# Retention heads on one Trainium2 core: six value and gate groups as seven-product pairs

## The chip, the cores and the metric

The kernel runs on one core of one Trainium2 chip. The core has a matrix engine (TensorE, PE in the profile, its weight loads PEld), VectorE (DVE), ScalarE (ACT), GpSimd (POOL) and SyncE (SP), which run side by side, each through its own queue in order. Transfers are issued from the queues of SP, ACT and POOL. The metric is the device time of one execution in microseconds (us), lower is better.

## The reference

A trunk of two layers over 256 tokens of width 2048: gated linear attention, then retention, each with a pre-norm, a gate path and a residual add, and a final norm. The change is in the retention layer:

```python
def retention_mixer(h, positions, w_in, gn_g, gn_b, w_out):
    proj = h @ w_in                       # 2048 -> 2048 q, 2048 k, 4096 v, 4096 gate
    q, k, v, gate = jnp.split(proj, [RET_DK, 2 * RET_DK, 2 * RET_DK + D_INNER], axis=-1)
    q, k = apply_rotary(q, cos, sin), apply_rotary(k, cos, sin)
    # 8 heads of 256 key and 512 value columns:
    #   o = (decayed causal scores of q, k) @ v, normed per head, * gn_g + gn_b
    return (o * jax.nn.silu(gate)) @ w_out
```

All of it is float32. The kernel keeps that precision by splitting each operand in two.

## The kernel before

**Split operands.** A number is held as a rounded high part `hi` and the rest `lo`. A product is three matmuls: high by high, high by `lo`, low by `hi`, each of 128 x 128 by 512 columns. Activations are held split for good: `xhl` (the normed layer input, transposed, 16 blocks of 128 of the contraction) and `ogt` (the gated head outputs). Weights are split as they stream in.

**Weights.** All weight matrices stand in `w_all` as groups of 512 columns, 16 blocks deep, in the order of use. `plan_all` lists once, ahead of the program, which chunks (4 blocks, 1024 KB, one load on SP into one of 4 `raw` buffers) and which units (2 blocks, half a chunk) are used in which order. `emit_split` splits one unit: ScalarE copies `raw` to `hi` (L207), VectorE writes `lo` = `raw` - `hi` (L208). `next_weights` keeps two units split ahead of the one in use; `hi` and `lo` have three buffers each.

**A head of retention** (`ret_head`) is three groups: `group_w` for the query and key columns (`rqk`), `group_x` for the value (`rv`) and for the gate (`rg`). `group_x` takes 8 units, each with 2 blocks x 2 token halves x 3 matmuls. `evac_w` copies the query/key sums out of PSUM (L411, L412), `ret_scores` makes rotary and scores, `o_mms` multiplies scores by values, a norm follows, `og_part` multiplies by the gate and `transpose_out` writes `ogt`. Heads 0 to 3 are followed by half of the output projection (`out_half`, `ra`), 4 to 7 by the other half (`rb`).

**Output halves** already use seven products. `pair_x` takes two groups of 512 columns at once. The first 8 of 16 blocks of the contraction form a 2 x 2 by 2 x 2 block product (two halves of the contraction, two token halves, two groups) which is made with 7 products (blocks S1 to S7, 2 units and 12 matmuls each) instead of 8; the other 8 blocks are done plainly (V0 to V3 for the first group, G0 to G3 for the second, 1 unit and 12 matmuls each). The sums of activations are made by `token_combos` on VectorE; the sums of weights are made by the transfer: once a unit of an S block is split, POOL issues a load of 512 KB that adds another chunk into the same `raw` buffer (L216). `join` adds a product into the residual tile `resid` as soon as it is done.

**Side work.** Generators in the queue `side` hold the work that isn't weights; `advance` runs one step of the first one after each unit or block, `drain_side` the rest. The order in each engine's queue is set by a scheduler when the program is built, from that order and from priorities. PSUM has 4 banks `acc`, 2 `lev`, 2 `mis`.

Of the kernel before, what the change touches and what calls it, by code (L numbers as in the profile page):

```python
# [17 lines left out]
P = 128  # L18
# [37 lines left out]
def kernel(  # L56
# [19 lines left out]
    one = pool("one", 1)  # L76
    raw_p = pool("raw", 4)
# [32 lines left out]
    def plan_units(c, last=True, then=()):  # L110
        for half in range(per_raw):
            units.append((c, half, last and half == per_raw - 1, then))
# [5 lines left out]
    PAIR = ("S1", "S2", "V0", "V1", "S5", "S3", "V2", "G0", "S6", "G1", "S7", "V3", "S4", "G2", "G3")  # L118

    def plan_pair(gp, gq):  # L120
# [7 lines left out]
        for block in PAIR:  # L128
            kind, n = block[0], int(block[1])
            if kind in "VG":  # L130
                j, half = divmod(n, 2)
                c = chunk(kind + str(j), gp if kind == "V" else gq, 2 + j)
                units.append((c, half, half == 1, ()))
            elif n == 2:
                plan_units(plan_chunk(gp, 1))
            elif n in (3, 7):
                plan_units(chunk("y", gq, 1), n == 7, [(gq, 0)] if n == 3 else ())
            else:
                then = {1: [(gq, 0)], 5: [(gq, 1)], 6: [(gp, 1)], 4: ()}[n]
                plan_units(chunk("x", gp, 0), n == 4, then)  # L140

    def plan_all():
        g = 0
        for stage, heads in (("gla", 2), ("gla", 2), ("ret", 4), ("ret", 4)):
            for _ in range(heads * (5 if stage == "gla" else 3)):
                plan_group(g)
                g += 1
            plan_pair(g, g + 1)
# [3 lines left out]
            else:  # L152
                plan_pair(g + 2, g + 3)
# [41 lines left out]
    def emit_split(pieces=1, between=None):  # L195
# [9 lines left out]
        for k in range(pieces):  # L205
            sl = slice(k * step, (k + 1) * step)
            a = nc.scalar.activation(hi[:, sl], src[:, sl], AF.Copy)  # L207
            b = nc.vector.tensor_tensor(lo[:, sl], src[:, sl], hi[:, sl].bitcast(F32), ALU.subtract)  # L208
            if i == 0:
# [4 lines left out]
        for g, k in then:  # L214
            rows = slice(j * SUB, (j + 1) * SUB)
            nc.gpsimd.dma_start(src, chunk_src(g, k)[:, rows], accum_op=ALU.add)  # L216
# [4 lines left out]
    state = {"sub": 0}  # L221
    side = deque()

    def advance(n=1):
        for _ in range(n):
            while side:
                try:
                    next(side[0])
# [37 lines left out]
    def product(ps, a, hi, lo, q, start, stop):  # L266
        xh, xl = a
        mm(ps, xh, hi[:, q, :], start=start, stop=False, skip_group_check=True)
        mm(ps, xh, lo[:, q, :], start=False, stop=False, skip_group_check=True)
        mm(ps, xl, hi[:, q, :], start=False, stop=stop, skip_group_check=True)  # L270

    def token_combos(lhs, name):
# [12 lines left out]
        for half in range(2):  # L285
# [9 lines left out]
            d = v_p.tile([P, 2, 2, CHUNK, P], F32R, tag="v", name=f"{name}_d{half}")  # L295
# [5 lines left out]

    combos = {}

    def pair_x(lhs, name, cname, join, done):

        a = lev_p.tile([P, GW], F32, tag="lev", name=f"{name}_psa")
        c11 = acc_p.tile([P, GW], F32, tag="acc", name=f"{name}_ps11")

        def seven(ps, get, start, stop):
            for half in range(2):  # L310
                hi, lo = next_weights()
                for q in range(SUB):
                    k = half * SUB + q
                    product(ps, get(k), hi, lo, q, start and k == 0, stop and k == CHUNK - 1)
# [5 lines left out]
        def mixed(n):  # L320
            return lambda k: tuple(x[:, k] for x in combos[cname][n])

        def both(ps, j, start, stop):
            hi, lo = next_weights()
            for q in range(SUB):
                for t in range(2):
                    kt = 2 * CHUNK + j * SUB + q
                    x = tuple(lhs[:, kt, i, t * P : (t + 1) * P] for i in range(2))
                    product(ps[t], x, hi, lo, q, start[t] and q == 0, stop[t] and q == SUB - 1)
            advance()  # L330

        c21 = b = c12 = c22 = None
        for block in PAIR:
            kind, n = block[0], int(block[1])
            if kind == "V":
                if c21 is None:
                    c21 = acc_p.tile([P, GW], F32, tag="acc", name=f"{name}_ps21")
                if n == 2:
                    drain_side()
                both((c11, c21), n, (False, n == 0), (n == 3, False))  # L340
                if n == 3:
                    done(0, 0, c11)
            elif kind == "G":
                if c22 is None:
                    c22 = lev_p.tile([P, GW], F32, tag="lev", name=f"{name}_ps22")
                both((c12, c22), n, (False, n == 0), (n == 3, n == 3))
                if n == 3:
                    done(0, 1, c12)
                    done(1, 1, c22)
            elif n == 1:  # L350
                seven(a, plain(0, 0), True, True)
                join(0, 0, a, ALU.add)
            elif n == 2:
                seven(c11, plain(1, 0), True, False)
            elif n == 5:
                while cname not in combos:
                    advance()
                b = lev_p.tile([P, GW], F32, tag="lev", name=f"{name}_psb")
                seven(b, mixed(0), True, True)
                join(0, 1, b, ALU.subtract)  # L360
                join(1, 1, b, ALU.add)
            elif n == 3:
                c12 = acc_p.tile([P, GW], F32, tag="acc", name=f"{name}_ps12")
                seven(c12, mixed(2), True, False)
            elif n == 6:
                seven(a, mixed(1), False, True)
                join(0, 1, a, ALU.subtract)
            elif n == 7:
                seven(a, mixed(3), False, True)
                join(1, 0, a, ALU.subtract)  # L370
                join(1, 1, a, ALU.add)
            elif n == 4:
                seven(c21, plain(1, 1), False, True)
                done(1, 0, c21)

    def group_w(rhs, name, extra=None):
        ps = [acc_p.tile([P, 2, SEQ], F32, tag="acc", name=f"{name}_ps{c}") for c in range(4)]
        for j in range(NSUB):
# [3 lines left out]
            if last:  # L382
# [19 lines left out]
            if extra is not None:  # L402
                extra(j)
            advance()
        return ps

    def evac_w(ps, dst, name):
        tmp = t4_p.tile([P, 4, SEQ], F32, tag="t4", name=f"{name}_h2")
        with tc.high_priority():
# [22 lines left out]
    resid = const([P, 2, D], "resid")  # L432
# [85 lines left out]
    def square_sum(t, c):  # L518
        junk = sg_p.tile([P, GW], F32, tag="sg", name="sqj")
        nc.scalar.activation(  # L520
            junk, resid[:, t, c * GW : (c + 1) * GW], AF.Square, accum_out=ssum[:, t, c : c + 1]
# [36 lines left out]
    def gate_low_rank():  # L558
        for t in range(2):
            keep(nc.sync.dma_start(resid[:, t, :], x_n[:, t, :]))  # L560
# [42 lines left out]
    def o_mms(sc, v, name):  # L603
        ps = [acc_p.tile([P, GW], F32, tag="acc", name=f"{name}_ps{t}") for t in range(2)]
# [11 lines left out]
    def transpose_out(src, kt0, scale0, dst, name):  # L616
        for half in range(2):
# [7 lines left out]
            for jj in range(2):  # L625
                kt = kt0 + half * 2 + jj
                if scale0 is None:
                    nc.scalar.activation(dst[:, kt, 0, :], tp[:, jj, :], AF.Copy)
                    nc.vector.tensor_tensor(
                        dst[:, kt, 1, :], tp[:, jj, :], dst[:, kt, 0, :].bitcast(F32), ALU.subtract  # L630
                    )
                else:
# [127 lines left out]
    def gla_head(h):  # L760
# [22 lines left out]
        def o_part(gi):  # L783
# [9 lines left out]
            if gi == 1:  # L793
                side.append(og_part(0))
                if h % 2:
                    side.append(token_combos(ogt, "gb" if h == 3 else "ga"))
# [48 lines left out]
    def out_cols(c, ps, t, first, final):  # L845
        dst = resid[:, t, c * GW : (c + 1) * GW]
# [8 lines left out]
    def out_half(first, final, name, later=None):  # L855
        def finish(t, c, ps):
# [3 lines left out]
            for _ in transpose_out(  # L860
                lambda t, j: resid[:, t, c * GW + j * P : c * GW + (j + 1) * P],
# [7 lines left out]
        for pair in range(1 if final else 2):  # L869
# [5 lines left out]
            def join(t, n, ps, op):  # L875
                c = 2 * pair + n
                dst = resid[:, t, c * GW : (c + 1) * GW]
                with tc.high_priority():
# [318 lines left out]
```

## Time and profile before

| what | value |
|---|---|
| median of 3 runs | 1400.7 us (1400.02 to 1400.75) |
| profiled execution, its own time | 1400.51 us |
| its span, first to last instruction | 1398.7 us |
| granted TensorE clock | 0.998 of full |
| TensorE busy / weight loads busy | 1385.4 us (99%) / 1163.1 us (83%) |
| VectorE, ScalarE, GpSimd busy | 999.6, 746.9, 100.0 us |
| HBM read / written | 285.51 MB / 2.10 MB |
| unit splits: L207 on ScalarE, L208 on VectorE | 515 each, 1058 and 1221 ns |

A row of a group reads: source line, engine, operation, output tile <- input tiles, shape, count | busy time in us, mean ns of one | idle time just before them and what ended it. Lines are those of the kernel before. Buffer numbers are left out of tile names.

### The profile page before, as it was taken

To read this page: it belongs to the slowest core of one execution; us is meant where nothing else is said; L and a number is where in the kernel's file an instruction comes from. 1 tells how busy PE (TensorE), PEld (TensorE's weight loads), DVE (VectorE), ACT (ScalarE), POOL (GpSimd) and SP (SyncE) were. 2 spreads that over 40 slices of the span, in tenths; PEclk is the share of its full clock that TensorE was granted. 3 is DMA by queue.
4 is the path that set the end of the run, shared out by engine and by line. 5 is a ranking of instruction groups with operands and counts; after the bars stand their busy time and mean duration, and the time that the engine had idled before them with its cause. 6 is when DMAs were issued, how large, how long until landed. Compare 5 with 4: busy or idle time off the path is not lost.

```text
span 1398.7 us, 17710 instructions
## 1 busy us (share of the span) xinstructions
PE 1385.4 (99%) x6716; PEld 1163.1 (83%) x6716; DVE 999.6 (71%) x1531; ACT 746.9 (53%) x954; POOL 100.0 (7%) x155
## 2 busy tenths in 40 slices
PE   8999999999999999999999999999999999999997
PEld 7888888788888888888888888888888888888887
DVE  6595798787845784887766666687766666668783
ACT  6665656655554646666444444456544444444563
POOL 1001030110010020111000000001100000000200
PEclk9999999999999999999999999999999999999999
DMA  9554555898555555799555555569975555555981
GB/s 365 196 181 150 191 182 180 199 298 261 178 179 181 178 194 183 193 281 281 184 191 189 191 190 190 182 195 269 265 250 179 201 181 200 183 200 177 232 298 60
DMA packets 47205, 288.75 MB, mean 206 GB/s; under 512 B 5632, under 2 KB 6144, under 8 KB 17296
## 3 DMA queue, kind: packets, MB, share of 16 engines
q1 hardware_dynamic: 35808, 249.71, 51.0%
q0 software_dynamic: 10304, 36.57, 13.2%
q10 hardware_dynamic: 1008, 1.35, 0.3%
q8 instruction: 52, 0.85, 0.2%
q14 instruction: 33, 0.27, 0.1%
HBM read 285.51 MB, written 2.10 MB: 206 GB/s over the span
## 4 chain that ended last, share of the span: by engine, by line
PE 98%; DVE 1%; ACT 1%; DMA 0%; issue 0%; ACTq 0%; DVEq 0%
PE rqk_ps L400 8%; PE gv_ps L247 4%; PE gg_ps L247 4%; PE gv_ps L248 4%; PE rv_ps L248 4%; PE rv_ps L249 4%; PE rv_ps L247 4%; PE gg_ps L248 4%; PE gv_ps L249 4%; PE gg_ps L249 4%; PE rg_ps L249 4%; PE rg_ps L248 4%; PE rg_ps L247 4%; PE rqk_ps L401 4%; PE gqk_ps L400 4%; PE gqk_ps L401 2%
## 5 line engine op out<-in xcount | busy, mean ns | idle before, releaser
L208 DVE TENSOR_TENSOR lo<-raw,hi 128x1024 fp32r<-128x1024 f32 (+1 forms) x515 | 623.9, 1221 | 307.7 <-ACT hi L207 305.3
L207 ACT ACTIVATE hi<-raw 128x1024 fp32r<-128x1024 f32 (+1 forms) x515 | 543.4, 1058 | 537.8 <-PE rg_ps L249 97.9
L400 PE MATMUL rqk_ps<-xhl,hi 128*128 128x512 f32 x480 | 167.3, 398 | 0.0
L401 PE MATMUL rqk_ps<-xhl,lo 128*128 128x256 f32 x480 | 127.3, 280 | 0.0
L400 PEld LDWEIGHTS rqk_ps<-xhl,hi 128*128 128x128 f32 x480 | 89.0, 188 | 18.0
L248 PE MATMUL rv_ps<-lo,xhl 128*128 128x512 f32 x256 | 100.4, 392 | 0.0
L248 PE MATMUL gv_ps<-lo,xhl 128*128 128x512 f32 x256 | 100.4, 392 | 0.0
L248 PE MATMUL gg_ps<-lo,xhl 128*128 128x512 f32 x256 | 100.4, 392 | 0.0
L249 PE MATMUL gv_ps<-hi,xhl 128*128 128x512 f32 x256 | 100.3, 392 | 0.0
L249 PE MATMUL gg_ps<-hi,xhl 128*128 128x512 f32 x256 | 100.0, 391 | 0.0
L249 PE MATMUL rv_ps<-hi,xhl 128*128 128x512 f32 x256 | 99.7, 390 | 0.0
L248 PE MATMUL rg_ps<-lo,xhl 128*128 128x512 f32 x256 | 99.6, 389 | 0.0
L249 PE MATMUL rg_ps<-hi,xhl 128*128 128x512 f32 x256 | 99.6, 389 | 0.0
L247 PE MATMUL gv_ps<-hi,xhl 128*128 128x512 f32 x256 | 93.0, 391 | 0.0
L247 PE MATMUL rg_ps<-hi,xhl 128*128 128x512 f32 x256 | 91.8, 389 | 0.0
L247 PE MATMUL gg_ps<-hi,xhl 128*128 128x512 f32 x256 | 91.7, 391 | 0.0
L247 PE MATMUL rv_ps<-hi,xhl 128*128 128x512 f32 x256 | 91.7, 390 | 0.0
L401 PEld LDWEIGHTS rqk_ps<-xhl,lo 128*128 128x128 f32 x480 | 89.1, 189 | 3.1
L400 PE MATMUL gqk_ps<-xhl,hi 128*128 128x512 f32 x216 | 72.4, 396 | 0.0
L216 POOL DMA_DIRECT2D raw<-in_w_all x56 | 48.3, 862 | 294.8 <-DVE lo L208 276.7
L248 PEld LDWEIGHTS rg_ps<-lo,xhl 128*128 128x128 f32 x256 | 48.0, 188 | 10.0
L247 PEld LDWEIGHTS rg_ps<-hi,xhl 128*128 128x128 f32 x256 | 48.1, 188 | 10.0
(412 smaller groups left out, 2482.9 us busy)
## 6 DMA issues: line engine op xcount, KB each, us to landing
raw<-in_w_all SPq DMA_DIRECT2D x231, 1024.0 KB, 4.9
raw<-in_w_all POOLq DMA_DIRECT2D x56, 512.0 KB, 7.4
resid<-in_x_n SPq DMA_DIRECT2D x2, 1024.0 KB, 10.9
gg<-in_gn_g POOLq DMA_DIRECT2D x8, 256.0 KB, 3.8
gb<-in_gn_b POOLq DMA_DIRECT2D x8, 256.0 KB, 4.5
raw<-in_w_all SPq DMA_DIRECT2D x3, 512.0 KB, 6.6
xt<-in_x_t SPq DMA_DIRECT2D x3, 512.0 KB, 8.2
dm<-in_dmat POOLq DMA_DIRECT2D x8, 192.0 KB, 2.7
```

The costliest lines, as they stand in the source:

```text
L207: a = nc.scalar.activation(hi[:, sl], src[:, sl], AF.Copy)
L208: b = nc.vector.tensor_tensor(lo[:, sl], src[:, sl], hi[:, sl].bitcast(F32), ALU.subtract)
L216: nc.gpsimd.dma_start(src, chunk_src(g, k)[:, rows], accum_op=ALU.add)
L247: mm(ps, xh, hi[:, q, :], start=kt == 0, stop=False)
L248: mm(ps, xh, lo[:, q, :], start=False, stop=False)
L249: mm(ps, xl, hi[:, q, :], start=False, stop=kt == NKT - 1)
L400: mm(ps[c], wh, rhs[:, kt, :, :], start=kt == 0, stop=False)
L401: mm(ps[c][:, 0, :], wl, rhs[:, kt, 0, :], start=False, stop=False)
```

## The change

In each half of the retention layer the first three heads (0 to 2 and 4 to 6) make value and gate together as one pair with seven products; heads 3 and 7 keep the two plain groups.

- `plan_all` and `plan_pair` list the chunks and units of those pairs, with an order of blocks `RET` that puts V0 ahead of S2.
- `token_combos` is also run on `xhl`, once in each half (`x1`, `x2`). Its split results stay for three heads in the buffer of the residual tile (`res_p`). For that time the residual (2048 KB) is stored to DRAM (`held`) at the end of the output half, from POOL, and loaded back in head 3 and head 7.
- `pair_x` gives each finished product to a handler `on`. For the heads the handler puts products into the `o` and `sg` tiles: S1, S5 and S7 are copied by ScalarE, the others added by VectorE. In output halves the product of S5 stays in its PSUM bank as the start of the fourth sum, which takes one `join` out of each of the seven pairs.
- The score-by-value product, the norm and the gate of a paired head move into the next head's query/key group (`late_o`, banks `lev`).
- From the first retention head on, each side step is queued behind the two latest split instructions (`behind_splits`), and the steps of `ret_scores` and of the norm are cut smaller. `transpose_out` evacuates two blocks in one instruction where there is no scale.

```diff
-    PAIR = ("S1", "S2", "V0", "V1", "S5", "S3", "V2", "G0", "S6", "G1", "S7", "V3", "S4", "G2", "G3")
+    OUT = ("S1", "S2", "V0", "V1", "S5", "S3", "V2", "G0", "S6", "G1", "S7", "V3", "S4", "G2", "G3")
+    RET = ("S1", "V0", "S2", "V1", "S5", "S3", "V2", "G0", "S6", "G1", "S7", "V3", "S4", "G2", "G3")
...
+            latest[:] = [a.ins, b.ins]
...
+    @contextmanager
+    def behind_splits():
+        with tc.issue_after(latest[0]), tc.issue_after(latest[1]):
+            yield
...
-                    next(side[0])
+                    with behind_splits() if state["behind"] else nullcontext():
+                        next(side[0])
...
-            d = v_p.tile([P, 2, 2, CHUNK, P], F32R, tag="v", name=f"{name}_d{half}")
+            d = room(half)
...
+    def room_res(name):
...
+                t.append(res_p.tile([P, 2, 2, 2, CHUNK, P], F32R, tag="resid", name=f"{name}_d"))
...
+        if keep_resid:
+            nc.gpsimd.dma_start(held, R["t"])
...
+        def on(event, ps, shared=True):
+            if event == "p1":
+                with tc.high_priority():
+                    nc.scalar.activation(o[:, 1, :], ps, AF.Copy)
+            elif event == "q":
+                with tc.high_priority():
+                    nc.scalar.activation(sg[:, 0, :], ps, AF.Copy)
+            elif event == "p2":
+                with tc.high_priority():
+                    tt(sg[:, 0, :], ps, sg[:, 0, :], ALU.add)
+            elif event == "p3":
+                with tc.high_priority():
+                    nc.scalar.activation(o[:, 0, :], ps, AF.Copy)
+            elif event == "11":
+                with tc.high_priority():
+                    tt(o[:, 1, :], ps, o[:, 1, :], ALU.add)
+                split_scaled(v[:, 0], o[:, 1, :], r2[:, 0:1])
+            elif event == "21":
...
+            else:
+                t = int(event[0]) - 1
+                with tc.high_priority():
+                    tt(sg[:, t, :], ps, (o if t else sg)[:, 0, :], ALU.add if t else ALU.subtract)
+                keep(nc.scalar.activation(sg[:, t, :], sg[:, t, :], AF.Silu, scale=r[:, t : t + 1]))
...
+        pair_x(xhl, f"rp{h}_", "x1" if h < 4 else "x2", on, RET)
...
+            new_resid(f"resid{h}")
+            nc.gpsimd.dma_start(R["t"], held)
...
-    out_half(False, False, "gb")
+    out_half(False, False, "gb", keep_resid=True)
+    side.append(token_combos(xhl, "x1", room_res("x1")))
     for h in range(4):
         ret_head(h)
-    out_half(True, False, "ra")
+    out_half(True, False, "ra", keep_resid=True)
+    side.append(token_combos(xhl, "x2", room_res("x2")))
```

The order on the engines, at three places. Tile numbers are those of each program, and brackets name what the instruction waits for. First, ScalarE where the query/key group of head 1 ends, before: `hi280` and `hi281` are the first two units of the value group, split ahead, `rqk1_h2` the copies of the query/key sums, `hi282` the value group's third unit.

```order
L207 ACTIVATE hi280_6313<-raw124_6227 128x1024 [waits DMAHW5_49,DVE_49,PE_49]
L207 ACTIVATE hi281_6333<-raw124_6227 128x1024 [waits DVE_49,PE_49]
L411 ACTIVATE rqk1_h2_6354<-rqk1_ps0_6161 128x256 [waits PE_49]
L411 ACTIVATE rqk1_h2_6354<-rqk1_ps1_6162 128x256 [waits PE_49]
L411 ACTIVATE rqk1_h2_6354<-rqk1_ps2_6163 128x256 [waits PE_49]
L411 ACTIVATE rqk1_h2_6354<-rqk1_ps3_6164 128x256 [waits PE_49]
L207 ACTIVATE hi282_6367<-raw125_6269 128x1024 [waits DMAHW6_49,DVE_49]
```

The same place now: `hi286` and `hi287` are the two units of S1, `hi288` is V0, `ogt` the copies of head 0's transposed output.

```order
L217 ACTIVATE hi286_6350<-raw123_6246 128x1024 [waits DMAHW4_49,DVE_49,PE_49]
L217 ACTIVATE hi287_6371<-raw123_6246 128x1024 [waits DVE_49,PE_49]
L455 ACTIVATE rqk1_h2_6393<-rqk1_ps0_6164 128x256 [waits PE_49]
L678 ACTIVATE ogt_107<-rot0_tp0_6314 128x2x256 [waits PE_49]
L678 ACTIVATE ogt_107<-rot0_tp1_6341 128x2x256 [waits PE_49]
L455 ACTIVATE rqk1_h2_6393<-rqk1_ps1_6165 128x256 [waits PE_49]
L455 ACTIVATE rqk1_h2_6393<-rqk1_ps2_6166 128x256 [waits PE_49]
L455 ACTIVATE rqk1_h2_6393<-rqk1_ps3_6167 128x256 [waits PE_49]
L217 ACTIVATE hi288_6412<-raw124_6292 128x1024 [waits DMAHW5_49,DVE_49]
```

The copies of the head before have moved between the query/key copies, ahead of the first unit behind S1. Second, TensorE at V2 of head 1's pair, a place that the program before doesn't have in a head: `hi295` is the last unit of S3, `hi296` V2 and `hi297` G0.

```order
L348 MATMUL rp1__ps12_6530<-lo295_6515,x1_d_5700 128x512
L349 MATMUL rp1__ps12_6530<-hi295_6514,x1_d_5700 128x512
L347 MATMUL rp1__ps11_6438<-hi296_6533,xhl_106 128x512 [waits Activation_49]
L347 MATMUL rp1__ps21_6439<-hi296_6533,xhl_106 128x512
L347 MATMUL rp1__ps12_6530<-hi297_6545,xhl_106 128x512 [waits Activation_49]
L347 MATMUL rp1__psb_6500<-hi297_6545,xhl_106 128x512
L348 MATMUL rp1__ps11_6438<-lo296_6534,xhl_106 128x512 [waits DVE_49]
```

Four matmuls by `hi` stand ahead of the first one by V2's `lo`; in the value group before, two do so (`hi282` and `lo282` are its third unit):

```order
L247 MATMUL rv1_ps0_6363<-hi282_6367,xhl_100 128x512 [waits Activation_49]
L247 MATMUL rv1_ps1_6364<-hi282_6367,xhl_100 128x512
L248 MATMUL rv1_ps0_6363<-lo282_6368,xhl_100 128x512 [waits DVE_49]
L249 MATMUL rv1_ps0_6363<-hi282_6367,xhl_100 128x512
L248 MATMUL rv1_ps1_6364<-lo282_6368,xhl_100 128x512
```

Third, ScalarE in the query/key group of head 4, whose units are `hi390` to `hi397` before:

```order
L207 ACTIVATE hi393_8551<-raw172_8447 128x1024 [waits DVE_49,PE_49]
L207 ACTIVATE hi394_8573<-raw173_8487 128x1024 [waits DMAHW6_49,DVE_49,PE_49]
L207 ACTIVATE hi395_8593<-raw173_8487 128x1024 [waits DVE_49,PE_49]
L207 ACTIVATE hi396_8615<-raw174_8529 128x1024 [waits DMAHW7_49,DVE_49,PE_49]
L207 ACTIVATE hi397_8635<-raw174_8529 128x1024 [waits DVE_49,PE_49]
```

and `hi408` to `hi415` now:

```order
L217 ACTIVATE hi411_8636<-raw169_8524 128x1024 [waits DVE_49,PE_49]
L217 ACTIVATE hi412_8661<-raw170_8565 128x1024 [waits DMAHW3_49,DVE_49,PE_49]
L308 ACTIVATE x2_d_8656<-x2_c0_8633 128x1024 [waits DMASW4_49,DVE_49]
L217 ACTIVATE hi413_8684<-raw170_8565 128x1024 [waits PE_49,Activation_49]
L308 ACTIVATE x2_d_8656<-x2_c1_8681 128x1024 [waits DVE_49]
L217 ACTIVATE hi414_8708<-raw171_8611 128x1024 [waits DMAHW4_49,PE_49,Activation_49]
```

The copies of the combinations `x2_d` stand among the splits, and the first of them waits for a transfer of POOL (`DMASW4`), the store of the residual.

More of the change, by code (lines that the diff above doesn't have):

```diff
@@ L126, in chunk @@
             return at[key]
-        for block in PAIR:
+        for block in order:
             kind, n = block[0], int(block[1])
@@ L313, in seven @@
                     k = half * SUB + q
-                    product(ps, get(k), hi, lo, q, start and k == 0, stop and k == CHUNK - 1)
+                    product(bank[key], get(k), hi, lo, q, start and k == 0, stop and k == CHUNK - 1)
             advance()
@@ L320, in mixed, with both @@
         def mixed(n):
+            while cname not in combos:
+                advance()
             return lambda k: tuple(x[:, k] for x in combos[cname][n])
-        def both(ps, j, start, stop):
+        def both(keys, j):
+            start = [take(key, acc_p, "acc") for key in keys]
+            stop = [left[key] == 1 for key in keys]
             hi, lo = next_weights()
@@ L328, in both @@
                     x = tuple(lhs[:, kt, i, t * P : (t + 1) * P] for i in range(2))
-                    product(ps[t], x, hi, lo, q, start[t] and q == 0, stop[t] and q == SUB - 1)
+                    product(bank[keys[t]], x, hi, lo, q, start[t] and q == 0, stop[t] and q == SUB - 1)
+            for key in keys:
+                wrote(key)
             advance()
-        c21 = b = c12 = c22 = None
-        for block in PAIR:
+        for block in order:
             kind, n = block[0], int(block[1])
[L335 to L349, printed above, removed]
+            if kind in "VG":
+                if block == "V2" and late is not None:
+                    late()
+                both(("11", "21") if kind == "V" else ("12", "22"), n)
@@ L350, in pair_x @@
             elif n == 1:
-                seven(a, plain(0, 0), True, True)
-                join(0, 0, a, ALU.add)
+                take("a", lev_p, "lev")
+                seven("a", plain(0, 0), True, True)
+                on("p1", bank["a"])
             elif n == 2:
-                seven(c11, plain(1, 0), True, False)
+                start = take("11", acc_p, "acc")
+                seven("11", plain(1, 0), start, left["11"] == 1)
+                wrote("11")
             elif n == 5:
-                while cname not in combos:
-                    advance()
@@ L358, in pair_x @@
[L358 to L361, printed above, removed]
+                get = mixed(0)
+                take("b", lev_p, "lev")
+                seven("b", get, True, True)
+                shared = "22" not in bank
+                on("q", bank["b"], shared)
+                if shared:
+                    bank["22"] = bank["b"]
             elif n == 3:
-                c12 = acc_p.tile([P, GW], F32, tag="acc", name=f"{name}_ps12")
@@ L370, in pair_x, with group_w @@
-                join(1, 0, a, ALU.subtract)
-                join(1, 1, a, ALU.add)
+                seven("a", mixed(3), False, True)
+                on("p3", bank["a"])
             elif n == 4:
-                seven(c21, plain(1, 1), False, True)
-                done(1, 0, c21)
-    def group_w(rhs, name, extra=None):
+                start = take("21", acc_p, "acc")
+                seven("21", plain(1, 1), start, left["21"] == 1)
+                wrote("21")
+    def group_w(rhs, name, extra=None, hook=None):
@@ L381, in group_w @@
             order = [(q, c) for q in range(SUB) for c in range(4)]
-            if last:
+            if last or (j == 0 and hook is not None):
                 order = [(q, c) for c in range(4) for q in range(SUB)]
@@ L1021, in ret_scores, with late_o @@
         box["sc"] = sc
+    waiting = []
     def ret_head(h):
         hw = {}
-        ps = group_w(xhl, f"rqk{h}")
+        paired = h % 4 < 3
+        def late_o(j):
+            if j == 0 and waiting:
+                waiting.pop()()
+        state["behind"] = True
+        ps = group_w(xhl, f"rqk{h}", hook=late_o)
         drain_side()
@@ L1030, in ret_head @@
         qk = t4_p.tile([P, 4, SEQ], F32, tag="qk", name=f"rqk{h}", bufs=1)
-        evac_w(ps, qk, f"rqk{h}")
+        with behind_splits() if paired else nullcontext():
+            evac_w(ps, qk, f"rqk{h}", not paired)
         hw["qk"] = qk
```

217 lines of the change are left out of this document (145 added, 72 removed).

## The prediction

> **What bounds the kernel now.** I read the page first (busy shares, then the chain that ended last), then the stages one by one.
>
> ```profile
> span 1398.7 us, 17710 instructions
> PE 1385.4 (99%) x6716; PEld 1163.1 (83%) x6716; DVE 999.6 (71%) x1531; ACT 746.9 (53%) x954; POOL 100.0 (7%) x155
> PE 98%; DVE 1%; ACT 1%; DMA 0%; issue 0%; ACTq 0%; DVEq 0%
> ```
>
> The chain runs over TensorE for 98% of the span. A busy TensorE need not be one at its peak, so its pace has to be seen: the first matmul of the first value group, the first of the gate group behind it, and 96 of 512 columns from one to the other.
>
> ```profile
> 34.96 0.39 PE L247 MATMUL gv_ps<-hi,xhl 128*128 128x512 f32 x1
> ...
> 56.74 0.39 PE L247 MATMUL gg_ps<-hi,xhl 128*128 128x512 f32 x1
> ```
>
> (56.74 - 34.96) / 96 = 0.227 us each, one behind the other. The 0.39 in a row is one matmul's length and overlaps with the next. Removing a matmul is worth 0.227 us as long as the weights arrive split in time. Whether they do is read by stage: one classic head of retention, then the two seven-product output pairs `ra`, which are the nearest thing in the trace to what the change builds. Columns: stretch, its length, busy time of each engine (count), granted clock, DMA share, GB/s.
>
> ```profile
> core 0: us, PE busy (x) PEld busy (x) DVE busy (x) ACT busy (x) POOL busy (x), PEclk, DMA share, GB/s
> 731.40:801.50 70.10, 70.10 (x348) 59.33 (x347) 46.55 (x67) 31.56 (x40) 1.61 (x3) 1.00 0.56 190
> 941.80:982.00 40.20, 40.20 (x182) 33.06 (x181) 32.05 (x35) 25.06 (x28) 6.33 (x8) 1.00 1.01 276
> 982.00:1025.00 43.00, 43.00 (x191) 35.38 (x191) 33.73 (x34) 23.55 (x23) 6.55 (x8) 1.00 1.01 283
> ```
>
> A classic head has slack everywhere but on TensorE. A seven-product pair has VectorE at 32 to 34 of 40 to 43 us and the DMA engines full, and yet lost almost nothing: over both pairs the weight loads waited for
>
> ```profile
> PEld ra_ps L269 <- DVE lo L208: 0.6, 3, 0.2
> ```
>
> 0.6 us, three times, at most 0.2. The form of work that the change puts into six heads therefore runs at TensorE's pace here, with little to spare.
>
> **Step 1, the matmuls taken out.** A value and a gate group hold 2 x 96 matmuls. A pair holds 7 products x 12 = 84 for the first half of the contraction and 96 for the other half: 180. Twelve fewer in each of six heads are 72, and the order of the changed program has 72 fewer of that shape and no other change in matmul shapes. 72 x 0.227 = **16.3 us off**, all on the path.
>
> **Step 2, what it adds to VectorE and ScalarE in a pair.** The durations, from the classic head above (count | busy, mean ns):
>
> ```profile
> L208 DVE TENSOR_TENSOR lo<-raw,hi 128x1024 fp32r<-128x1024 f32 x24 | 29.3, 1223 | 18.7 <-ACT hi L207 18.7
> L412 DVE TENSOR_TENSOR rqk<-rqk_ps,rqk_h 128x256 f32<-128x256 f32 x4 | 1.5, 418 | 0.0
> L592 DVE SCALAR_TENSOR_TENSOR rv<-rv_ps,r,rv 128x512 fp32r<-128x512 f32 x2 | 1.4, 751 | 0.4 <-ACT rv L591 0.4
> L994 DVE TENSOR_TENSOR ra<-rqk,trig 128x1024 f32<-128x1024 f32 x1 | 1.2, 1224 | 0.0
> L998 DVE TENSOR_TENSOR ra<-ra,rb 128x512 f32<-128x512 f32 x1 | 0.7, 684 | 0.0
> L1018 DVE TENSOR_TENSOR rs<-rs,dm 128x384 f32<-128x384 f32 x1 | 0.6, 557 | 0.5 <-PE rs L1015 0.5
> L207 ACT ACTIVATE hi<-raw 128x1024 fp32r<-128x1024 f32 x24 | 25.4, 1059 | 33.4 <-PE rg_ps L249 13.1 <-PE rqk_ps L400 9.8 <-PE rv_ps L249 7.7
> L600 ACT ACTIVATE rsg<-rg_ps,r 128x512 f32<-128x512 f32 x3 | 2.1, 690 | 2.0 <-PE rg_ps L249 2.0
> L411 ACT ACTIVATE rqk_h<-rqk_ps 128x256 f32<-128x256 f32 x4 | 1.5, 379 | 0.8 <-PE rqk_ps L398 0.8
> ```
>
> A pair splits 22 weight units instead of 16. VectorE then has 22 x 1.223 = 26.9 us of splits; five joins of 128x512 (as L998, 0.684) and two scaled splits (L592): 4.9; the scores (L994, five of 0.684, 0.418 and two of 0.557): 6.2; the query/key evacuation (4 x 0.418) and two merged transpose evacuations (0.684 each): 3.0. That is 41.0 us against 180 x 0.227 = 40.9 and 0.9 of score matmuls (4 x 128 and 6 x 256 columns at that pace), some 42. Back to back they overlap, which the next rows show: three splits took 3.49, not 3.67. With 0.08 off each of its 44 operations the queue needs about 38 of 42 us, where the output pair needs 33. It still fits; the question is the waits in order. ScalarE has 22 x 1.059 = 23.3 and sixteen others of 0.4 to 0.7, some 32 of 42.
>
> How the loop closes (start, length, what ended the idle time), inside `ra`:
>
> ```profile
> 954.02 2.20 ACT L207 ACTIVATE hi<-raw 128x1024 fp32r<-128x1024 f32 x2 [1.84 <-PE ra_ps L270]
> 956.51 1.06 ACT L207 ACTIVATE hi<-raw 128x1024 fp32r<-128x1024 f32 x1 [0.30 <-PE ra_psb L270]
> ...
> 955.11 2.36 DVE L208 TENSOR_TENSOR lo<-raw,hi 128x1024 fp32r<-128x1024 f32 x2 [1.67 <-ACT hi L207]
> 957.39 1.28 DVE L879 TENSOR_TENSOR resid<-resid,ra_psb 128x512 f32<-128x512 f32 x2
> 958.59 3.49 DVE L208 TENSOR_TENSOR lo<-raw,hi 128x1024 fp32r<-128x1024 f32 x3
> ```
>
> With three `hi` buffers, unit i cannot be split before TensorE leaves unit i-3; `lo` starts 1.09 after `hi` (954.02, 955.11) and lasts 1.22. I allow 0.35 us from the start of the next unit to ScalarE's start (0.39 - 0.23 for the matmul's tail, the rest for the signal). A V or G unit lasts 12 matmuls, 2.72 us, a unit of an S block half of that. After two S units the margin is 2.72 + 0.45 (two `hi` matmuls stand ahead of the first `lo` one) - 0.35 - 1.09 - 1.22 = 0.5 us, and whatever stands between on ScalarE must be shorter.
>
> *Query/key to pair (V0 behind S1; the first place of the order).* With S1 starting at 0 and a query/key unit of 2.8 us ahead of it (below), ScalarE finishes the last early `hi` at -2.8 + 0.35 + 1.06 = -1.4, does one query/key copy (0.38) to -1.0, the two merged transpose copies (0.69 each, the nearest 512-column row, L600) to 0.36, and three more query/key copies to 1.5. V0's `hi` runs 1.5 to 2.56, its `lo` 2.6 to 3.8, and is due at 2.72 + 0.45 = 3.17: 0.65 late. Heads 1, 2, 5 and 6 have the transposes there; 0 and 4 come behind an output half, have none, and are in time by the same working (`hi` from 0.73, `lo` done at 3.05). 4 x 0.65 = 2.6. Ends: 0 if the copies get in earlier; 4 x 1.22 = 4.9 if a whole split is late.
>
> *V2 behind S5 and S3 (second place).* ScalarE copies the S5 product (0.69, urgent) before the `hi` of V2 and G0, so these come about 0.7 later than in the output pair, where VectorE takes that product. TensorE's order has four `hi` matmuls, 0.9 us, ahead of V2's `lo`, which pays for the rest; I take 0.25 a pair, 6 x 0.25 = 1.5. Ends: 0, and 6 x 0.7 = 4.2 if nothing covers it.
>
> *Transfers in a pair.* Eight accumulating loads of 512 KB are added to each pair. Output pairs do the same, at the share 1.01 above, without starving TensorE; the query/key group between pairs runs at the classic 0.56. I cost them at nothing: what hides them is the three blocks, 8.2 us, and the two units of look-ahead between a block's split and its reuse, against 7.4 us to landing (below). If that goes, the next S block's `hi` is late.
>
> *The output halves* lose one join on VectorE in each of seven pairs, where they waited 0.3 us a pair (0.6 over two, above): take 0.5 off in all, ends 0 and 2.
>
> **Step 3, the residual's way out and back.** The page has for transfers (KB each, us to landing):
>
> ```profile
> raw<-in_w_all SPq DMA_DIRECT2D x231, 1024.0 KB, 4.9
> raw<-in_w_all POOLq DMA_DIRECT2D x56, 512.0 KB, 7.4
> out<-resid SPq DMA_DIRECT2D x4, 256.0 KB, 2.6
> ```
>
> A 2048 KB store from POOL is not in the trace. From 256 to 1024 KB cost 2.3 us more, so alone it lands after 4.9 + 1024/334 = 8.0; four times the accumulating load gives 29.6. Nearest is the plain load, shared with one or two weight loads of about 3.1 us each that the query/key group brings meanwhile: I take 12. It is issued 1.8 us after that group begins (two last joins), so it lands at 13.8.
>
> It matters because the combinations take over the residual's buffer, and their ScalarE copy stands in the middle of the query/key splits (third place). A query/key unit takes 2.8 us:
>
> ```profile
> 1030.26 0.92 PE rqk_ps L400 x4
> ...
> 1033.06 0.93 PE rqk_ps L400 x4
> ```
>
> In head 4 the copy stands ahead of the sixth unit's `hi`. That unit is due at 5 x 2.8 = 14.0; with copy, VectorE's half and the split behind it, 1.1 + 1.14 + 1.22 ahead, the copy must start at about 10.5. Landing at 13.8 makes **3.3 us** of stall. In head 0 it stands ahead of the eighth unit, two units later, with 16 transposes in between: due about 17.9, so nothing. Ends: 0 (8.0 + 1.8 is under 10.5); with 29.6, landing at 31.4, 20.9 + 13.5. The DMA page of the Trainium skill (DMA: Bandwidth & Descriptors, section Anatomy of one DMA) fits a POOL transfer as 2.0 us plus bytes over 436 GB/s. By that the store would take an estimated 6.8 us, the stall would vanish and the whole come to about 1388. It would give an estimated 3.2 us for the 512 KB loads, where the trace has 7.4 beside other traffic, so I don't lean on it here.
>
> The load back, in heads 3 and 7, has the value and gate groups of 24 us each ahead of its first use: nothing, unless it delays weights at a pair's end. The 7.6 us of combinations a half (4 x 1.22 + 4 x 0.684) lie in the query/key group, whose eight units need only 9.8 of 22 us on VectorE.
>
> **Sum.** -16.3 + 2.6 + 1.5 + 3.3 - 0.5 = -9.4 us. The profiled execution took 1400.5 us, 0.2 under the median 1400.7: **1391 us**. A measurement of this kernel tells 0.2%, 2.8 us, from no change.
>
> **Rivals.** (B) *Every wait is hidden*: 1400.5 - 16.3 - 0.5, 1384 to 1387. For it: the output pairs' 0.6 us. Against: 38 instead of 33 us on VectorE. (C) *VectorE becomes the pair's bound, and it ends slower*. In the two `ra` pairs its splits idled 16.6 us for ScalarE's `hi`, 8.3 a pair:
>
> ```profile
> L208 DVE TENSOR_TENSOR lo<-raw,hi 128x1024 fp32r<-128x1024 f32 x44 | 52.7, 1221 | 17.0 <-ACT hi L207 16.6
> ```
>
> If that idling belongs to the loop, and isn't slack, a pair takes 38 + 8.3 = 46 us, 4 over its matmuls: 6 x 4 on top gives 1400.5 - 16.3 + 3.3 - 0.5 + 24 = 1411. It ends slower from about 2.2 us a pair on ((16.3 - 3.3)/6). Against it: V and G units leave VectorE 1.5 us each. (D) *The store takes the accumulating load's pace*: 20.9 + 13.5 in place of 3.3, 1422; it ends slower from about 18 us to landing. (E) *Partly either*: 5 to 9 us more than I have, 1396 to 1400. That the products aren't removed at all is excluded by the order's count.
>
> **Chances.** Forecast 0.60 (its own range 1387 to 1395), B 0.13, C 0.09, D 0.06, E 0.12. Faster: the first two and two thirds of E, and a little of C's mild end, 0.83; same 0.06; slower 0.11. The range leaves out the best of B and, above 1399, most of C and D: 1385 to 1399.
>
> **What would show it.** Step 1: matmuls of 512 in the page's count down by 72, a paired head near 67 us, granted clock still 1.00. Step 2: weight loads of the pairs wait for VectorE's `lo`, under 1.5 us a pair, first at V0 of heads 1, 2, 5, 6; VectorE busy near 38 to 40 us in a pair. Step 3: one wait of 2 to 5 us in head 4's query/key group, ended by the store, none in head 0's. Wrong: waits above 2 us in each pair, waits of `hi` for accumulating loads, or a store over 18 us.

## The result, and the profile after

The changed kernel took 1387.6 us, the median of four runs (1387.2 to 1389.8), against 1400.7 for the kernel before on the same chip (1400.0 to 1401.8). The ratio is 0.991, 95% interval 0.989 to 0.993: 13.1 us faster, 3.4 us more than the likeliest case of the forecast (1391), inside its range and 0.6 us above what it gave as the end of case B (1384 to 1387). The profiled execution took 1387.69 us, its span is 1385.9; between the two profiled executions the span fell by 12.8.

The page after, the same three lines as before:

```profile
span 1385.9 us, 17829 instructions
PE 1371.7 (99%) x6644; PEld 1150.2 (83%) x6644; DVE 1064.3 (77%) x1590; ACT 793.7 (57%) x996; POOL 144.2 (10%) x207
PE 91%; DMA 4%; DVE 2%; issue 2%; ACT 1%; POOL 0%; ACTq 0%; POOLq 0%; DVEq 0%
```

TensorE has 72 matmuls fewer (6716 to 6644) and is still busy for 99%. The chain now runs for 4% over transfers, where it had 0%: the weights come with less to spare.

By stage, the columns as in the forecast: head 1 as a whole (70.1 us before), its pair alone, and the two `ra` pairs.

```profile
core 0: us, PE busy (x) PEld busy (x) DVE busy (x) ACT busy (x) POOL busy (x), PEclk, DMA share, GB/s
728.01:795.52 67.51, 67.51 (x336) 57.16 (x335) 55.91 (x77) 38.95 (x46) 8.55 (x11) 1.00 0.83 242
752.06:795.24 43.18, 43.18 (x197) 35.90 (x196) 36.72 (x42) 27.79 (x34) 5.82 (x8) 1.00 0.94 262
934.10:974.60 40.50, 40.46 (x182) 32.93 (x181) 34.23 (x41) 24.66 (x26) 6.66 (x9) 1.00 0.99 273
974.60:1017.70 43.10, 43.10 (x192) 35.59 (x191) 33.30 (x33) 23.68 (x23) 6.79 (x8) 1.00 1.01 275
```

Head 1 takes 67.5 us: 2.6 us less, where twelve matmuls are worth 2.72. VectorE is busy 36.7 of 43.2 us in the pair and the DMA engines 0.94; the clock stayed at 1.00.

What the weight loads of the retention layer waited for (sum, times, longest):

```profile
PEld rp__ps L348 <- DVE lo L218: 1.5, 3, 0.7
PEld ra_ps L348 <- DVE lo L218: 0.8, 2, 0.5
PEld rb_ps L348 <- DVE lo L218: 0.8, 2, 0.5
PEld rqk_ps L442 <- ACT hi L217: 0.7, 1, 0.7
PEld rqk_ps L442 <- DVE xhl L470: 0.6, 1, 0.6
```

In the six pairs (`rp`) they waited three times, 1.5 us together: in S4, the last S block, of heads 4 and 6, and 0.3 at V0 of head 0. Some 0.04 us of each such wait is the usual pause between two weight loads (one takes 0.188 us, at a pace of 0.227); the losses given for single blocks below leave it out. The two `rqk` waits are at the start of head 7's query/key group and near the end of head 0's.

Where the 12.8 us of the span came from, from the starts of the groups in both traces: all that comes ahead of head 0 became 0.6 us shorter; heads 0 to 3 7.1 (of 8.2 for 36 matmuls); heads 4 to 7 6.0 (of 8.2); `ra` 0.5 longer, and `rb` with the end 0.4 longer.

### The profile page after: what moved, and what is told of

The parts are those of the page before. It is cut to its first block, busy times and chain, and to the rows that moved or that the text cites. A ratio compares the mean times of both kernels' runs of the same rounds, so it can differ in the third digit from the quotient of the medians.

```text
span 1385.9 us, 17829 instructions
## 1 busy us (share of the span) xinstructions
PE 1371.7 (99%) x6644; PEld 1150.2 (83%) x6644; DVE 1064.3 (77%) x1590; ACT 793.7 (57%) x996; POOL 144.2 (10%) x207
## 4 chain that ended last, share of the span: by engine, by line
PE 91%; DMA 4%; DVE 2%; issue 2%; ACT 1%; POOL 0%; ACTq 0%; POOLq 0%; DVEq 0%
PE rqk_ps L442 7%; PE gv_ps L265 4%; PE gg_ps L265 4%; PE gv_ps L267 4%; PE gg_ps L267 4%; PE gg_ps L266 4%; PE gv_ps L266 4%; DMA raw<-in_w_all 4%; PE gqk_ps L442 4%; PE rqk_ps L443 4%; PE rp__ps L348 3%; PE rp__ps L349 3%; PE rp__ps L347 3%; PE gqk_ps L443 2%; PE ra_ps L348 1%
## 5 line engine op out<-in xcount | busy, mean ns | idle before, releaser
L217 ACT ACTIVATE hi<-raw 128x1024 fp32r<-128x1024 f32 (+1 forms) x551 | 581.4, 1058 | 501.0 <-PE gg_ps L267 67.9
L218 DVE TENSOR_TENSOR lo<-raw,hi 128x1024 fp32r<-128x1024 f32 (+1 forms) x551 | 669.2, 1223 | 252.7 <-ACT hi L217 245.5
L227 POOL DMA_DIRECT2D raw<-in_w_all x104 | 89.6, 862 | 465.3 <-DVE lo L218 408.8
L348 PE MATMUL rp__ps<-lo,xhl 128*128 128x512 f32 x192 | 75.2, 392 | 0.4 <-DVE lo L218 0.4
L349 PE MATMUL rp__ps<-hi,xhl 128*128 128x512 f32 x192 | 74.8, 390 | 0.0
L347 PE MATMUL rp__ps<-hi,xhl 128*128 128x512 f32 x192 | 70.0, 390 | 0.0
L803 POOL TENSOR_TENSOR s<-s,m 128x64 f32<-128x64 f32 x56 | 32.3, 610 | 240.9 <-DVE m L794 230.2
L266 PEld LDWEIGHTS gv_ps<-lo,xhl 128*128 128x128 f32 x256 | 48.1, 188 | 9.6
L266 PEld LDWEIGHTS gg_ps<-lo,xhl 128*128 128x128 f32 x256 | 48.1, 188 | 9.6
L267 PEld LDWEIGHTS gg_ps<-hi,xhl 128*128 128x128 f32 x256 | 48.1, 188 | 9.6
L265 PEld LDWEIGHTS gv_ps<-hi,xhl 128*128 128x128 f32 x256 | 47.9, 188 | 9.8
```

The lines of the kernel that those rows point to most:

```text
L227: nc.gpsimd.dma_start(src, chunk_src(*then)[:, rows], accum_op=ALU.add)
L265: mm(ps, xh, hi[:, q, :], start=kt == 0, stop=False)
L266: mm(ps, xh, lo[:, q, :], start=False, stop=False)
L267: mm(ps, xl, hi[:, q, :], start=False, stop=kt == NKT - 1)
L803: nc.gpsimd.tensor_tensor(dst, dst, side_of(m[:, li, :]), ALU.add)
```

## The experiments

Each edit is made to the changed kernel, and all times stand beside runs of the kernel before on the same chip (1400.4 to 1400.8 in each set).

**One pair in each half.** Only heads 0 and 4 are paired; the others keep two plain groups.

```diff
-                if stage == "ret" and h < heads - 1:
+                if stage == "ret" and h < 1:
...
-        paired = h % 4 < 3
+        paired = h % 4 < 1
```

> Only heads 0 and 4 are pairs; the others keep two plain groups. Theory A (the gain is the matmuls taken out, and almost all waits are hidden): two heads of six, 24 matmuls of 0.227 us, 5.4 us off 1400.7, with the combinations and the residual's store still paid (0.5 us in head 0's query/key group): about 1395.5. Theory B (a good part of the gain comes from the reordered side work, not from the pairs): under 1392.

1396.8 us (1396.0 to 1398.6), ratio 0.998 (0.997 to 0.999): 1.3 more than theory A gave, and far from B.

**No pairs.** No head is paired, and so nothing is stored and no combinations of `xhl` are made; the queueing, the small steps, the merged copies and the S5 product that stays in its bank are kept.

> No head is a pair, nothing is stored or combined for the heads; the side work in small steps behind the splits, the merged transpose copies and the output pairs with one join less stay. Theory A: the gain is the pairs', so this is the kernel before less the 0.9 us that the first two output halves gained: 1399 to 1401. Theory B (side work behind splits is worth something by itself): 1397 or less. A rival on the other side: the norm steps of heads 3 and 7 now reach into the output halves, which lost 0.5 us each, so 1401 to 1402.

1400.5 us (1399.4 to 1402.0), ratio 1.000 (0.999 to 1.001). All the rest of the change together is worth nothing by itself. With two pairs it is 3.7 us less, 1.8 a pair; with six 12.8, 2.1 a pair, where twelve matmuls are 2.72. The gain is the matmuls taken out, with about a fifth lost.

**Not behind the splits.** Side steps are put into the queues where the program reaches them, without the wait for the two latest splits, and the query/key sums are copied out as in the plain heads.

```diff
-        state["behind"] = True
+        state["behind"] = False
...
-        with behind_splits() if paired else nullcontext():
-            evac_w(ps, qk, f"rqk{h}", not paired)
+        with nullcontext():
+            evac_w(ps, qk, f"rqk{h}")
```

> All six pairs, but side steps and the query/key sums are no longer queued behind the latest splits; the sums are urgent, as in the kernel before. Theory A (VectorE has 36.7 of 43.2 us in a pair, and a unit's slack is about half a microsecond behind two S units, 2 us behind V and G): an operation of 0.7 us ahead of a split costs some tenths where it stands behind S units, 0.5 to 1.5 us a pair: 1390 to 1396. Theory C (the queueing is not needed, since VectorE has room): 1387 to 1388.5.

1397.5 us (1393.7 to 1399.1), ratio 0.998 (0.997 to 0.999): 9.9 us slower than the changed kernel, more than either theory gave. Waits of its weight loads in the pairs, then VectorE in head 4, whose S1 begins at 1047.3 (start, length, what ended the idle time):

```profile
PEld rp__ps L348 <- DVE lo L218: 9.4, 11, 1.8
...
1045.69 1.23 DVE L218 TENSOR_TENSOR lo<-raw,hi 128x1024 fp32r<-128x1024 f32 x1 [0.99 <-ACT hi L217]
1046.83 1.53 DVE L456 TENSOR_TENSOR rqk<-rqk_ps,rqk_h 128x256 f32<-128x256 f32 x4
1048.40 1.23 DVE L1061 TENSOR_TENSOR ra<-rqk,trig 128x1024 f32<-128x1024 f32 x1
1049.54 0.69 DVE L1063 TENSOR_TENSOR rb<-rqk,trig 128x512 f32<-128x512 f32 x1
1050.14 0.69 DVE L1065 TENSOR_TENSOR rb<-rqk,trig 128x512 f32<-128x512 f32 x1
1050.74 2.35 DVE L218 TENSOR_TENSOR lo<-raw,hi 128x1024 fp32r<-128x1024 f32 x2
```

9.4 us in place of 1.5. Three steps of the scores, 2.3 us together, ran ahead of V0's `lo` at 1050.74, and V0 waited 1.7 us for it, as in head 0; heads 1, 2, 5 and 6 lost 0.9 each in S2 instead, and heads 2, 4 and 5 another 0.3 to 1.3 at G2. VectorE has time enough in a pair, but not at any moment: with the same work in another order most of the gain is gone. Some 4 us of the loss are not in the pairs: in `ra` the weight loads waited 2.9 us, where the changed kernel has 0.8, first for a unit whose load landed late, and seven matmuls behind that ran at half the pace. Why that load was late is not shown.

**S2 ahead of V0.** The heads' pairs take the order of blocks of the output pairs (`OUT` in place of `RET`).

> The heads' pairs in the order of the output pairs: S2 directly behind S1, then V0, V1. Theory A: four S units in a row stand behind the query/key group, each needing a split in 1.36 us where VectorE takes 1.14 and the query/key sums come on top (four copies and four adds, 0.9 to 1.4 us): 0.5 to 1.2 us of wait at the second S2 unit or V0 in each pair, 3 to 7 us in all: 1391 to 1395. Theory C: no difference, 1387 to 1388.5.

1390.0 us (1389.5 to 1391.5), ratio 0.993 (0.992 to 0.995): 2.3 us slower than `RET`, between the two theories. The pairs' waits:

```profile
PEld rp__ps L348 <- DVE lo L218: 4.8, 12, 0.6
```

V0 then waits 0.55 us in each of the heads 1, 2, 4, 5 and 6, behind the two short units of S2.

**The transposed copies twice.** Each merged copy of the transposed output (L678) is written a second time, which adds two copies on ScalarE at the start of the pairs of heads 1, 2, 5 and 6, ahead of V0.

> ScalarE writes each merged transpose copy of the retention heads twice, the same values. Two copies of 0.55 us more stand between the query/key copies and the hi of V0 in heads 1, 2, 5 and 6. Theory A (the loop as the forecast worked it, with the trace's start of that hi at 0.48 us behind S1's start, not 1.5): hi at 1.55, its lo done at 3.9, due at 3.2: 0.7 us of wait at V0 in each of the four heads, up to 0.5 at the starts of the output halves, 3 us slower, 1390.5. Rival (the slack is larger than half a microsecond): no change, 1387.5.

1391.7 us (1390.2 to 1393.1), ratio 0.994 (0.992 to 0.995): 4.1 us slower, where theory A gave 3 and its rival nothing. ScalarE where the group of head 1 ends; first the changed kernel, whose S1 begins at 752.29:

```profile
748.70 1.06 ACT L217 ACTIVATE hi<-raw 128x1024 fp32r<-128x1024 f32 x1 [1.76 <-PE rqk_ps L442]
750.43 0.38 ACT L455 ACTIVATE rqk_h<-rqk_ps 128x256 f32<-128x256 f32 x1 [0.67 <-PE rqk_ps L440]
751.00 1.09 ACT L678 ACTIVATE ogt<-rot_tp 128x512 fp32r<-128x512 f32 x2 [0.19 <-PE rot_tp L673]
751.97 0.94 ACT L455 ACTIVATE rqk_h<-rqk_ps 128x256 f32<-128x256 f32 x3
752.77 2.16 ACT L217 ACTIVATE hi<-raw 128x1024 fp32r<-128x1024 f32 x2
```

then with the copies twice, S1 from 752.46:

```profile
751.16 1.09 ACT L678 ACTIVATE ogt<-rot_tp 128x512 fp32r<-128x512 f32 x2 [0.18 <-PE rot_tp L673]
...
752.40 0.62 ACT L679 ACTIVATE ogt<-rot_tp 128x512 fp32r<-128x512 f32 x1
...
753.14 0.64 ACT L679 ACTIVATE ogt<-rot_tp 128x512 fp32r<-128x512 f32 x1
...
753.88 2.06 ACT L217 ACTIVATE hi<-raw 128x1024 fp32r<-128x1024 f32 x2
```

The last row of each is V0's `hi`. It starts 0.48 us after S1 in the changed kernel, where V0 doesn't wait, and 1.42 after S1 here, where V0 waits 0.87 in each of the four heads. If each further delay of `hi` is a delay of V0, V0 stays in time up to 1.42 - 0.87 = 0.55: the changed kernel makes it by about 0.1 us.

**No store.** The residual isn't stored at the end of the output half; heads 3 and 7 load an input of the same size in its place, so that the residual of the layers before is missing.

```diff
-            nc.gpsimd.dma_start(held, R["t"])
+            pass
...
-            nc.gpsimd.dma_start(R["t"], held)
+            nc.gpsimd.dma_start(R["t"], x_n)
```

> The residual's store is left out, and heads 3 and 7 load the kernel's input in its place (same size); the combinations stand where they stood. It leaves out the residual of the layers before. Theory A (the combination's copy stands ahead of the eighth unit of the query/key group, due some 16 us into it, and the store lands 10 to 12.6 us into it): nothing, 1387.5 within 0.7. The forecast's term (due at 10.5 us): 3 us faster, 1384.5.

1387.9 us (1386.2 to 1389.0), ratio 0.990 (0.989 to 0.992). The same as with the store: it costs nothing that these times show, and the 3.3 us of the forecast are excluded.

**The store twice.** A second store of the same data waits behind the first, on the same queue.

> The store of the residual is issued twice, one behind the other, so that the combinations get its buffer later. Theory A (the unit was miscounted: the copy stands ahead of the eighth unit in head 4 as in head 0, and is due about 15.4 us after the query/key group begins, since lo413 had 2.9 us to spare in the changed kernel): landing 22 to 24 us after the group's start in head 4, a wait of 7 to 8 us; 19 to 20 in head 0, a wait of about 4; whole 1397 to 1400. Theory B (the forecast's working: due at 10.5 in head 4 and 17.9 in head 0): a wait of 12 to 13 us in head 4 and 1 to 2 in head 0; whole 1401 to 1403.

1397.4 us (1395.0 to 1402.3), ratio 0.999 (0.997 to 1.000). The total is A's, but the place is neither theory's: in this program the copies of the combinations do not stand among the query/key splits, but behind the last split of S1 in head 4 and just ahead of it in head 0, where S1 and V0 lost 1.7 us. In head 4 the second store landed late, and the copies, and behind them V0's `hi`, began at

```profile
1043.90 2.00 ACT L308 ACTIVATE x_d<-x_c 128x1024 fp32r<-128x1024 f32 x2 [5.11 <-DMA held<-resid]
1045.81 1.19 ACT L455 ACTIVATE rqk_h<-rqk_ps 128x256 f32<-128x256 f32 x4
1046.87 2.02 ACT L217 ACTIVATE hi<-raw 128x1024 fp32r<-128x1024 f32 x2
```

and V0 waited 5.1 us for `hi` and 1.4 for `lo`. So the run shows what a late store does, but doesn't tell the two readings of the changed kernel's order apart; that is read from the trace below. Behind that wait TensorE was slow for a while. The stretch and the one after it:

```profile
1050.50:1053.20 2.70, 2.70 (x8) 2.11 (x7) 2.70 (x4) 0.00 (x0) 0.00 (x0) 0.50 0.00 0
...
1054.00:1058.00 4.00, 4.00 (x20) 3.25 (x19) 2.44 (x3) 3.07 (x3) 0.00 (x0) 1.00 1.01 293
```

The granted clock was 0.50 and one matmul of 512 columns came every 0.427 us; then it was 1.00 again.

**The load back from SP, later.** SP issues it in the gate group of heads 3 and 7, where POOL issued it at the end of the pair before.

> The residual is loaded back from the queue of SP, in order behind the weight loads of the gate group of heads 3 and 7, instead of from POOL at the end of the pair before. Theory A (the load back slows the weight and accumulating loads at the end of head 6's pair, where 0.55 and 0.67 us were lost; head 2's lost nothing): 0.7 to 1.2 us faster, 1386.5 to 1387. Rival (the accumulating loads are late by themselves, as in head 4's pair, which has no load back): no change, 1387.5.

1387.1 us (1386.2 to 1388.0), ratio 0.990 (0.989 to 0.992): 0.5 less than the changed kernel, which the runs can't tell from nothing. In its profile the wait in head 7's query/key group (0.7 above) is gone, and so are those at S4 of heads 4 and 6, but three waits in the pairs of heads 0 to 2, 0.3 to 0.7 us (one of them at S4 of head 1), and 0.4 more in `ra` make up for them.

**Weights loaded one chunk later** (`DMA_LOOK` 1 in place of 2).

> Weight chunks are asked for one chunk ahead instead of two, everywhere. Theory D (the accumulating loads land late, 9 instead of 7.4 us, because the weight loads that run ahead share the DMA engines with them): the waits of hi for accumulating loads in the pairs shrink from 24 us in all, the 1.2 us lost in heads 4 and 6 vanish, 1386 to 1387. Rival E (one chunk ahead leaves too little time, 2.7 to 5.6 us for a load of 5 to 9 us): waits for weight loads everywhere, slower by 10 us or more.

1389.0 us (1386.0 to 1390.0), ratio 0.991 (0.990 to 0.993), no clear difference, and neither theory's size. In head 1's pair SP issues its first three loads 6.3, 8.0 and 25.8 us after S1 begins with either value: when a `raw` buffer comes free decides there, and not how far SP's queue may run ahead.

**Half of the weight sums.** In the heads' pairs the accumulating loads carry one of two blocks, so that half of the weight sums is left out.

> In the heads' pairs each accumulating load adds only 1 of 2 blocks (256 KB in place of 512); half of the weight sums is left out. Theory A (the waits of 0.5 to 0.9 us at S4 or V2 in one or two pairs, 1.2 to 1.5 us a run, come from transfers that land late because the DMA engines are full): share in a pair from 0.95 to about 0.8, no such wait in any pair, 1385.8 to 1387. Theory B (they come from the order on POOL or on the split engines): the waits stay, 1387 to 1388.

1386.1 us (1385.6 to 1387.6), ratio 0.989 (0.988 to 0.991): 1.6 less than the changed kernel, with ranges that overlap a little. Head 1's pair:

```profile
753.60:796.80 43.20, 43.20 (x198) 35.91 (x197) 36.78 (x42) 27.75 (x34) 5.92 (x8) 1.00 0.76 214
```

The share fell from 0.94 to 0.76, and no S4 waits in any pair. One wait of 1.0 us at V2 of head 0 stays, so A holds for S4 and not for V2, which waits for a plain load; the changed kernel's own profile has no wait there, while those of six other versions have one of 0.5 to 1.2. Whether the sums for S4 land in time because the engines are less full or because they are half the size themselves, the run doesn't tell.

**S4 one block later.** S4 and G2 change places, so that the sum for S4 has 2.7 us more.

```diff
-    RET = (... "S7", "V3", "S4", "G2", "G3")
+    RET = (... "S7", "V3", "G2", "S4", "G3")
```

> In the heads' pairs S4 and G2 change places, so that the sum for S4 has one block, 2.7 us, more to land. Theory A (S4 waits for its sum): no wait at S4, those at V2 stay, 1386 to 1387.2. Theory B (the last product's additions crowd the end of the pair): weight loads of the next query/key group or G3 wait 0.3 us or more a pair, 1388 to 1391.

1403.1 us (1396.6 to 1404.7), ratio 1.001 (1.000 to 1.002): 15.5 us slower than the changed kernel, which neither theory allowed. S4 no longer waits; G2 does, in all six pairs, 13.8 us together. The waits of the weight loads, then ScalarE and the clock in head 2:

```profile
PEld rp__ps L347 <- ACT hi L217: 9.6, 7, 2.1
PEld rp__ps L348 <- DVE lo L218: 5.9, 7, 1.0
...
858.83 1.06 ACT L217 ACTIVATE hi<-raw 128x1024 fp32r<-128x1024 f32 x1 [4.93 <-DMA raw<-in_w_all]
...
861.00:865.00 4.00, 3.81 (x10) 2.98 (x11) 3.76 (x5) 1.99 (x3) 0.00 (x0) 0.57 1.01 432
```

The plain load for G2 and G3 is issued 25.8 us after S1 begins in both kernels (845.6 and 849.9 in head 2), when a `raw` buffer comes free, and lands 8.5 to 8.8 later. With S4 ahead of it G2 is just in time; one block earlier it is 2.1 us late in head 2, and its `lo` another 1.0. Waits of 15.5 us in the pairs, and matmuls at half the clock behind those of heads 2 and 5, are more than the gain of the pairs. So both loads at the end of a pair stand within about one block of their due time: to give time to one takes it from the other.

## Why the prediction was right, and where it was not

**Step 1 (-16.3)** held: 72 matmuls fewer, head 1 2.6 us shorter, clock 1.00. That the pairs, and not the reordered side work, make the gain was argued there; the run without pairs (1400.5) shows it.

**V0 behind S1 (+2.6)** is nearly nothing: no wait in heads 1, 2, 5 and 6, and 0.2 us in head 0, where I had none. The term was mis-sized by the times put into a loop that is itself right, as the run with the copies twice shows. The eight transposes on TensorE lengthen the last query/key unit by about 1 us, so the last early `hi` started 3.6 us ahead of S1 where I had 2.45; each merged copy took 0.55, not 0.69. `hi` of V0 started 0.48 after S1, not 1.5. On the other side V0 was due earlier than I had: the bound is 0.55, while my working gives 2.56 - 1.06 - 0.65 = 0.85. Had the copies come as late as I said, the cost would have been 4 x 0.95.

**V2 (+1.5)**: no wait in this profile. The four `hi` matmuls ahead of its `lo` cover it; the nearest row, the `ra` pairs' waits, was the better guide. What other versions lose there in head 0 is a late load, not the S5 copy that I had costed.

**The store (+3.3)** fails on a miscount. In head 4 the copies stand ahead of the eighth unit's `hi`, as in head 0, not ahead of the sixth: the units of that group are `hi406` to `hi413`, and `hi414` and `hi415`, which the text ahead of the forecast counts to it, are already S1 (before, too, they are `hi388` to `hi395`). The due time was about 16 us after the group's start, not 10.5. Transfers after (KB each, us to landing) and ScalarE in head 4, whose group starts at 1017.69:

```profile
raw<-in_w_all SPq DMA_DIRECT2D x225, 1024.0 KB, 5.0
raw<-in_w_all POOLq DMA_DIRECT2D x104, 512.0 KB, 7.8
held<-resid POOLq DMA_DIRECT2D x2, 2048.0 KB, 10.1
resid<-held POOLq DMA_DIRECT2D x2, 2048.0 KB, 11.7
...
1030.39 1.06 ACT L308 ACTIVATE x_d<-x_c 128x1024 fp32r<-128x1024 f32 x1 [0.80 <-DMA held<-resid]
1031.40 1.06 ACT L217 ACTIVATE hi<-raw 128x1024 fp32r<-128x1024 f32 x1
```

The store landed after 8.9 us in head 0 and 11.4 in head 4, near my 12: 12.6 us into the group. ScalarE waited 0.8 us for it, TensorE not at all. The 6.8 us estimated from the fit of the Trainium skill's page (DMA: Bandwidth & Descriptors, Anatomy of one DMA) are too short for a transfer that shares the engines with weight loads; no stall, which followed from that estimate, came true for another reason, the due time.

**Transfers in a pair, costed at nothing**, are where the pairs do lose. The sums land later than before (7.8 against 7.4 over the whole kernel, a median of 9.1 in head 4's pair), and `hi` of S4 waits for one:

```profile
1073.19 2.09 ACT L217 ACTIVATE hi<-raw 128x1024 fp32r<-128x1024 f32 x2 [1.53 <-DMA raw<-in_w_all]
```

0.6 us each in heads 4 and 6; profiles of other versions show the like wait at S4 of head 1. Waits of `hi` for accumulating loads I had named as a sign of being wrong. The cover that I named, three blocks, is there, but used up to the last microsecond, as the run with S4 later shows. In head 6 the load back makes the first unit of head 7's group late, 0.7: that unit's load took 10.9 us, and 9.4 at the same place in head 2, against 6.9 to 7.5 in heads 0, 1, 4 and 5, and 7.2 and 7.6 in heads 6 and 2 of the run that loads the residual back later. That term I had mentioned and not priced.

**The combinations in head 0**, also costed at nothing, cost 0.5: there the norm's transposes of `xhl` (L469, L470) and the combinations meet on both split engines. In head 4, without the norm, they cost nothing.

**The output halves (-0.5)** came out at +0.7: `ga` and `gb` are 0.2 shorter together, `ra` and `rb` 0.9 longer; their first units now wait 0.8 us each half. The run without pairs has the same two waits at the start of `ra` and `rb`, so they come with the rest of the change and not with the pairs.

The sum by what was measured: -16.3 + 0.2 (V0) + 1.2 (S4) + 0.7 (load back) + 0.5 (combinations) + 0.7 (output halves) = -13.0, against -12.8. The first group of the kernel, which the change doesn't touch, is 0.5 shorter as well, so some 0.7 of loss isn't found. Terms too high by 2.4, 1.5 and 3.3 stood against 2.4 that I had costed at nothing and 1.2 in the output halves. That the total came within 3.4 us of the forecast is therefore luck in part: errors of 7.2 one way and 3.6 the other. The waits that I had priced were hidden nearly as rival B said, but others, which B had not either, took their place. Rival C had VectorE's idling for `hi` as part of the loop: with VectorE at 36.7 of 43.2 us, no wait in three pairs and 0.2 to 0.6 us in the others it was slack, but only as long as the queue keeps the splits first (the run not behind the splits). D falls with the store at 11 us.

## What to carry to other kernels

A product with fewer matmuls pays in full only where the weights still arrive in time, so work out the arrival by the place of each block in the order, from the issue of its load to its due time; an engine's busy share said nothing of the 10 us and 15 us that two reorderings cost. Count the units in the queue from the tiles that TensorE reads, not from the numbers at hand. With the DMA engines at 0.95, a block that was moved up lost the cover of its own load.

## What the runs showed of the hardware

Waits on TensorE can cost more than their length. In four places seven to ten matmuls came every 0.427 us in place of 0.227, at a granted clock down to 0.50, some 1.5 to 2.5 us on top: after waits of 6.5 us in the run with two stores, of 3.1 in head 2 and 2.5 in head 5 of the run with S4 later, and of 2.9 in `ra` of the run not behind the splits. After 3.0 us in head 1 and 2.4 in head 4 of the run with S4 later nothing of the kind followed, so the length of the waits alone doesn't decide. It differs between executions of one program too: of the twelve with S4 later, three had a mean granted clock of 0.998 or 0.999 and took 1396.6 to 1400.1 us, nine had 0.994 to 0.997 and took 1401.5 to 1404.7.

The Trainium skill (TensorE: Matmul & The Clock Gate, Part 1) says that the clock halves after an idle window of about 3.4 us and that this window runs free of the kernel. The half rate agrees, and that like waits have different consequences fits a window that runs free; but two waits of 1.5 and 1.0 us with two matmuls between them were enough.
